# A hybrid decoder trunk on one core: the order of every engine planned by a list scheduler, and four blocks of seven products per feed-forward

## The chip, the core and the metric

The kernel runs on one core of a Trainium2 chip. A core has a matrix engine (TensorE, in the profile PE, with weight loads as PEld), a vector engine (VectorE, DVE), a scalar engine (ScalarE, ACT), GpSimd (POOL) and SyncE (SP), each with an instruction queue of its own that runs strictly in order, and 16 DMA engines. Work on one engine waits for another by semaphores. The metric is the device time of one execution in microseconds, the median of several runs.

## What is computed

Two layers. Each normalizes, runs a SwiGLU feed-forward, adds half of its normalized result, runs a mixer of three head groups in parallel, adds its normalized result, and runs a second feed-forward. Everything is float32: 256 tokens, width 1,024, feed-forward width 2,816.

```
for l in range(2):
    f = swiglu(rmsnorm(h, ff1_norm_pre[l]), ff1_w_gate[l], ff1_w_up[l], ff1_w_down[l])
    h = h + 0.5 * rmsnorm(f, ff1_norm_post[l])
    m = hybrid_mixer(rmsnorm(h, mix_norm_pre[l]), w_in[l], ...)   # state space | pooling | attention, then w_out
    h = h + rmsnorm(m, mix_norm_post[l])
    f = swiglu(rmsnorm(h, ff2_norm_pre[l]), ff2_w_gate[l], ff2_w_up[l], ff2_w_down[l])
    h = h + 0.5 * rmsnorm(f, ff2_norm_post[l])

swiglu(h, wg, wu, wd) = (silu(h @ wg) * (h @ wu)) @ wd
```

Most of the work is the four feed-forwards, three matrices of 1,024 x 2,816 each.

## The kernel before

**Float32 by three passes.** Each float32 operand is split into a high part `hi` (a copy rounded to the matrix engine's fast float32 type, made by ACT, line 104) and a low part `lo` = raw - hi (made by DVE, line 105). A product is hi x hi + hi x lo + lo x hi, three matmuls. Activations are split once; every weight is split once too, so ACT and DVE touch each weight that PE uses.

**Units, jobs and buffers.** Weights come in units of 128 x 2,048 float32 (1 MB). `Weights.load` (line 77) issues a unit's load from SP into one of four `raw` buffers; a job (`split_next`) makes a `hi` and a `lo` tile from it in two pieces of 1,024 columns (four of 512 for the first units), with five such pairs of tiles. `pump`, called at chosen points of the program, loads and splits ahead as long as buffers are free, and thereby sets the order on SP, ACT and DVE; the order of PE is that of the program.

**The feed-forward.** The 2,816 columns are eleven blocks of 256. Blocks 0 and 1 (`FIRST`) are made row tile by row tile (128 tokens) while the norm of the second row tile is still under way. Blocks 4, 7 and 10 (`PAIRS`) are plain: gate and up, 48 matmuls with 256 columns each (`mm_feat`, line 300). The blocks 2-3, 5-6 and 8-9 (`QUADS`) use a product of two-by-two blocks with seven multiplications in place of eight: with the tokens in two halves and the width in two halves, `ffn_quad` makes seven products of 12 matmuls with 512 columns (`product`, line 430) and combines them with a few additions of PSUM banks (lines 451 to 472). Its weights are g1 (gate, upper half of the rows), g2 (gate, lower half), u1 and u2 (up), and sums of them: T1 = g1 + u1, T2 = T1 + u2, T3 = u1 + u2, T4 = T2 + g2. T1, T2 and T4 are made by DVE in place in g1's raw buffer (line 101); for T3 the unit u2 is loaded a second time from POOL, by a DMA that adds to what lies in u1's buffer (line 103). The result h0, h1 comes with tokens on partitions and is turned by PE transposes (`turn_h`, line 405); a pair's result needs no turning. After each block the down product of the blocks before it runs (`mm_rows`, line 336: 12 matmuls with 512 columns for a unit and row tile).

**The mixer** is a chain of many smaller steps on all engines between products with `w_in` and `w_out`.

**What sets the order.** Instructions are recorded in program order, and each engine runs its own in that order, but where `tc.issue_after` moves a few at the start.

Of the kernel before, what the change touches and what calls it, by code (L numbers as in the profile page):

```python
# [17 lines left out]
P = 128  # L18
# [28 lines left out]

class Weights:
# [3 lines left out]
    def __init__(self, nc, rawp, splitp):  # L52
        self.nc, self.rawp, self.splitp = nc, rawp, splitp
        self.units, self.raw, self.jobs, self.parts = [], {}, [], {}
        self.loaded = self.live = self.split = self.held = 0

    def unit(self, src, cols=UNIT):
        self.units.append((src, cols))
# [8 lines left out]
    def plan(self, src, cols=UNIT, pieces=2):  # L67
        u = self.unit(src, cols)
        return self.job(u, free=(u,), pieces=pieces)

    def load(self, pieces=1):
        i = self.loaded
        src, cols = self.units[i]
        t = self.rawp.tile([P, KD * QDT], F32, tag="raw", name=f"raw{i}")
        step = cols // pieces
        for c in range(0, cols, step):
            self.nc.sync.dma_start(t[:, c : c + step], src[:, c : c + step])
        self.raw[i] = t
        self.loaded += 1
        self.live += 1  # L80

    def ready(self):
        u, sum_of = self.jobs[self.split][:2]
        return max(u, *(sum_of[::2] if sum_of else (u,))) < self.loaded

    def split_next(self, only=None):
# [4 lines left out]
        if i not in self.parts:  # L91
            self.parts[i] = [self.splitp.tile([P, KD * QDT], F32R, tag=x, name=f"{x}{i}") for x in ("hi", "lo")]
        hi, lo = self.parts[i]
        step = cols // pieces
        for c in range(0, cols, step):
            if only and c // step not in only:
                continue
            s = slice(c, c + step)
            if sum_of:
                x, op, y = sum_of  # L100
                nc.vector.tensor_tensor(raw[:, s], self.raw[x][:, s], self.raw[y][:, s], op=op)  # L101
                if add and c + step == cols:
                    nc.gpsimd.dma_start(self.raw[add[0]][:, :cols], add[1], accum_op=ALU.add)
            nc.scalar.activation(hi[:, s], raw[:, s], AF.Copy)  # L104
            nc.vector.tensor_tensor(lo[:, s], raw[:, s], hi[:, s].bitcast(F32), op=ALU.subtract)  # L105
# [32 lines left out]
def hybrid_trunk_kernel(ctx: ExitStack, tc: tile.TileContext, a, out: bass.AP):  # L138
    nc = tc.nc
    consts = ctx.enter_context(tc.tile_pool(name="consts", bufs=1))  # L140
    rawp = ctx.enter_context(tc.tile_pool(name="rawp", bufs=RAW_BUFS))
    splitp = ctx.enter_context(tc.tile_pool(name="splitp", bufs=SPLIT_BUFS))
    tmp = ctx.enter_context(tc.tile_pool(name="tmp", bufs=1))
    small = ctx.enter_context(tc.tile_pool(name="small", bufs=6))
    psum = ctx.enter_context(tc.tile_pool(name="psum", bufs=4, space=bass.MemoryType.PSUM))

    ids = iter(range(10**6))

    def buf(dtype=F32, n=512, tag="t"):
# [48 lines left out]
    gains = consts.tile([P, 2, D], F32, name="gains")  # L198
    xT = [consts.tile([P, KD, S], F32R, name=f"xT{i}") for i in range(2)]
# [5 lines left out]
    def split_into(dst, at, src_f32):  # L205

        hi, lo = dst[0][at], dst[1][at]
        split_into.last = nc.scalar.activation(hi, src_f32, AF.Copy)  # L208
# [867 lines left out]
```

## Time and profile before

| what | us |
|---|---|
| median of 3 runs | 950.46 (949.59 to 950.59) |
| the profiled execution | 950.96 |
| its span, first to last instruction | 949.3 |
| the last two matmuls of the program start | 942.5 |

The profile tells of one execution. A group row reads: line, engine, operation, tiles written and read (buffer numbers left out), shapes, count, then busy time and mean duration of one in ns, and the idle time before it with what ended it. A timeline row has the start, the length from the first start to the last end, and the count of merged equal instructions; in brackets the idle time just before it. Instructions of one engine overlap in their last part, so n equal ones in a row take n - 1 steps and one duration, and a step is shorter than a duration.

### The profile page before, as it was taken

The page shows a single profiled execution, that of the slowest core. Times are in us where ns is not written, and L with a number is a line of the kernel's source. Part 1 is how long each engine was busy: PE and PEld are TensorE (multiplying, and loading weights), DVE is VectorE, ACT ScalarE, POOL GpSimd, SP SyncE. Part 2 cuts the span into 40 slices and gives each one's busy share as a digit, 9 for nine tenths or more (in the row PEclk, how much of TensorE's full clock was granted, in tenths as well). Part 3 has the DMA queues.
Part 4 walks back from the last instruction along what each step waited for, and adds up shares of the span by engine and source line. Part 5 has one row for each costly group of instructions (what it writes and reads, how often), then busy time and mean ns, then how long its engine had stood idle before and what let it go on. Part 6 is the DMA issues. An engine that isn't in the chain of part 4 may idle for free.

```text
span 949.3 us, 13147 instructions
## 1 busy us (share of the span) xinstructions
PE 929.7 (98%) x5066; PEld 794.9 (84%) x5066; DVE 789.8 (83%) x1067; ACT 580.5 (61%) x923; POOL 34.7 (4%) x47
## 2 busy tenths in 40 slices
PE   7999999999999999999999999999999999999997
PEld 4779898988988789898887888898898887989896
DVE  6899898588887998998589989786888799989772
ACT  7576656468737565747467666556685566665651
POOL 0000000010001000000010000000000110000000
PEclk9999999999999999999999999999999999999999
DMA  8667666656243476758454958583733263858531
GB/s 315 214 243 244 241 203 248 242 175 224 96 177 124 110 297 198 294 145 307 179 186 124 346 143 310 139 313 126 268 132 133 89 195 123 331 175 285 172 117 45
DMA packets 28003, 190.56 MB, mean 201 GB/s; under 512 B 3106, under 2 KB 3362, under 8 KB 5924
## 3 DMA queue, kind: packets, MB, share of 16 engines
q1 hardware_dynamic: 26212, 177.13, 51.0%
q0 software_dynamic: 1728, 12.58, 7.2%
q8 instruction: 40, 0.66, 0.3%
q14 instruction: 23, 0.19, 0.1%
HBM read 188.65 MB, written 1.05 MB: 200 GB/s over the span
## 4 chain that ended last, share of the span: by engine, by line
PE 71%; DVE 11%; ACT 7%; issue 4%; POOL 1%; DMA 1%; POOLq 0%; DVEq 0%; ACTq 0%
PE acc L336 25%; PE wk L430 22%; PE wk L300 18%; DVE lo L105 5%; ACT hi L104 2%; PE wk L319 2%; ACT n L225 2%; POOL s L219 1%; DVE raw L101 1%; PE wk L405 1%; ACT n L669 1%; DMA raw<-in_ff_q 1%; DVE xT L209 1%; DVE n L209 1%; PE wk L866 1%
## 5 line engine op out<-in xcount | busy, mean ns | idle before, releaser
L105 DVE TENSOR_TENSOR lo<-raw,hi 128x1024 fp32r<-128x1024 f32 (+2 forms) x440 | 468.1, 1102 | 62.5 <-ACT hi L104 61.9
L104 ACT ACTIVATE hi<-raw 128x1024 fp32r<-128x1024 f32 (+2 forms) x440 | 399.4, 959 | 176.9 <-PE wk L300 37.5
L336 PE MATMUL acc<-hi,t 128*128 128x512 f32 x832 | 221.5, 396 | 3.0 <-ACT hi L104 2.9
L336 PEld LDWEIGHTS acc<-hi,t 128*128 128x128 f32 x832 | 154.3, 189 | 37.4 <-ACT hi L104 3.7
L300 PE MATMUL wk<-xT,hi 128*128 128x256 f32 x1088 | 144.0, 285 | 0.0
L300 PEld LDWEIGHTS wk<-xT,hi 128*128 128x128 f32 x1088 | 136.8, 192 | 2.3 <-issue 0.7
L336 PE MATMUL acc<-lo,t 128*128 128x512 f32 x416 | 115.4, 391 | 1.5 <-DVE lo L105 1.5
L319 PE MATMUL wk<-hi,xT 128*128 128x512 f32 x384 | 102.1, 398 | 2.5 <-ACT xT L208 1.4
L430 PE MATMUL wk<-hi,n 128*128 128x512 f32 x384 | 100.4, 390 | 0.0
L336 PEld LDWEIGHTS acc<-lo,t 128*128 128x128 f32 x416 | 77.9, 188 | 19.2 <-DVE lo L105 2.8
L319 PEld LDWEIGHTS wk<-hi,xT 128*128 128x128 f32 x384 | 71.8, 190 | 20.5 <-ACT hi L104 3.1
L101 DVE TENSOR_TENSOR raw<-raw,raw 128x1024 f32<-128x1024 f32 x72 | 86.3, 1217 | 1.7 <-DMA raw<-in_ff_q 1.6
L430 PEld LDWEIGHTS wk<-hi,n 128*128 128x128 f32 x384 | 71.9, 188 | 15.5 <-issue 0.8
L430 PE MATMUL wk<-hi,xT 128*128 128x512 f32 x288 | 76.9, 391 | 0.0
L300 PE MATMUL wk<-xT,lo 128*128 128x256 f32 x544 | 76.9, 284 | 0.0
L300 PEld LDWEIGHTS wk<-xT,lo 128*128 128x128 f32 x544 | 70.3, 192 | 0.0
L430 PEld LDWEIGHTS wk<-hi,xT 128*128 128x128 f32 x288 | 53.8, 188 | 11.1
L319 PE MATMUL wk<-lo,xT 128*128 128x512 f32 x192 | 52.9, 396 | 1.0 <-DVE lo L105 1.0
L208 ACT ACTIVATE t<-wk 128x256 fp32r<-128x256 f32 x72 | 26.9, 375 | 42.0 <-DVE t L209 22.1
L430 PE MATMUL wk<-lo,n 128*128 128x512 f32 x192 | 51.3, 389 | 0.0
L233 DVE TENSOR_TENSOR n<-acc,gains 128x512 f32<-128x512 f32 x24 | 16.5, 688 | 35.9 <-ACT n L225 35.9
L319 PEld LDWEIGHTS wk<-lo,xT 128*128 128x128 f32 x192 | 36.1, 189 | 9.8 <-DVE lo L105 2.2
(172 smaller groups left out, 763.1 us busy)
## 6 DMA issues: line engine op xcount, KB each, us to landing
raw<-in_ff_q SPq DMA_DIRECT2D x48, 1024.0 KB, 5.0
raw<-in_ff_d SPq DMA_DIRECT2D x44, 1024.0 KB, 5.1
raw<-in_ff_f SPq DMA_DIRECT2D x16, 1024.0 KB, 5.7
raw<-in_ff_q POOLq DMA_DIRECT2D x12, 1024.0 KB, 8.0
raw<-in_ff_g SPq DMA_DIRECT2D x12, 1024.0 KB, 4.8
raw<-in_ff_u SPq DMA_DIRECT2D x12, 1024.0 KB, 5.0
raw<-in_w_in SPq DMA_DIRECT2D x10, 1024.0 KB, 4.9
raw<-in_w_kvz SPq DMA_DIRECT2D x8, 1024.0 KB, 6.2
```

The lines of the kernel that those rows point to most:

```text
L101: nc.vector.tensor_tensor(raw[:, s], self.raw[x][:, s], self.raw[y][:, s], op=op)
L104: nc.scalar.activation(hi[:, s], raw[:, s], AF.Copy)
L105: nc.vector.tensor_tensor(lo[:, s], raw[:, s], hi[:, s].bitcast(F32), op=ALU.subtract)
L208: split_into.last = nc.scalar.activation(hi, src_f32, AF.Copy)
L209: nc.vector.tensor_tensor(lo, src_f32, hi.bitcast(F32), op=ALU.subtract)
L219: nc.gpsimd.tensor_tensor(r, v, halfexp, op=ALU.pow)
L225: nc.scalar.activation(junk, x, AF.Square, scale=1.0 / (gain * math.sqrt(n)), accum_out=ssq)
L233: nc.vector.tensor_tensor(fg[i], f[i], gains[:, 1, i * 512 : (i + 1) * 512], op=ALU.mult)
L300: nc.tensor.matmul(ps, w[:, k, s], y[:, k, :], start=i == 0 and k == 0, stop=i == 2 and k == KD - 1)
L319: m = nc.tensor.matmul(ps, y[:, k, :], w[:, k, :], start=h == 0 and n == 0, stop=h == 1 and n == len(parts) - 1)
L336: nc.tensor.matmul(acc[b], x[:, j, s], w[:, j, b * 512 : (b + 1) * 512], start=first and j == 0 and i == 0, stop=last and j == 1 and i == 2)
L430: nc.tensor.matmul(ps, x[:, k, :], w[:, k, :], start=first and n == 0, stop=n == len(parts) - 1, skip_group_check=not first)
```

## The change

**Planned order.** The program is no longer issued as it is written. All engine calls go to a `Planner`, which notes for each which tiles (and which parts of them) it reads and writes, gives it a cost by formulas, and then runs a list scheduler over all five engines at once: it repeatedly takes the engine whose next choice starts first, and of that engine's ready operations (within 20 ns of the earliest) the one with the earliest due time. Due times run backwards from the time at which PE would need each operation if PE ran without a gap in program order. It also hands out the buffers. The kernel then emits the plan; `pump` and its look-ahead are gone.

**Blocks.** `QUADS` becomes (2, 4, 6, 8) and `PAIRS` (10,): four blocks of seven products and one pair in each feed-forward. In a block the order is g1, T1, g2, a down unit, T3, T2, a down unit, u2, T4. T2 is made like T3, by an accumulating load: after T1 is split, u2 is loaded onto it. So u2 is read three times, T1 and T4 remain additions on DVE.

**Pieces and buffers.** Splits and additions are done in one piece of 2,048 columns, but for the first units of a stage. Pairs of split tiles go from five to six, the 512-wide working buffers `t` from 22 to 14.

```diff
-RAW_BUFS = 4
-SPLIT_BUFS = 5
+PEKEY = 0
+PAD = 300.0
+TMP, NBUF, ROUNDS = 14, 8, 1
+RAW_BUFS = 4
+PF, FINE = 2, 'g1 T1 g2'.split()
+AHEAD = "".split()
+ORDER = "g1 0 T1 1 g2 d T3 T2 d u2 T4".split()
+SUMMED = "T3 T2".split()
+SPLIT_BUFS = 6
 TAIL = 4
-FIRST, QUADS, PAIRS = (0, 1), (2, 5, 8), (4, 7, 10)
+FIRST, QUADS, PAIRS = (0, 1), (2, 4, 6, 8), (10,)
...
+class Planner:
...
+    def arrange(self, target=None):
...
+        for o in reversed(ops):
+            o.late = -1e9 if o.rush else min([target.get(o.n, end)] + [q.late - g for q, g in post[o.n]])
...
+        def pick(e):
+            best = [(s, o) for o in hand[e] if (s := earliest(o)) is not None]
...
+            first = min(s for s, _ in best)
+            now = [(o.n if e == "tensor" and PEKEY else o.late, o.n, s, o) for s, o in best if s <= first + 20]
+            late, _, s, o = min(now)
...
+            if o.kind == "dma":
+                line = max(s + (600 if e == "sync" else 1500), line) + o.tail * (1 if e == "sync" else 1.5)
+                done = line + o.tail * (0 if e == "sync" else 0.5) + 1700.0
...
 class Weights:
...
-    def job(self, unit, sum_of=None, free=(), pieces=2, add=None):
+    def job(self, unit, sum_of=None, free=(), pieces=1, add=()):
...
-                if add and c + step == cols:
-                    nc.gpsimd.dma_start(self.raw[add[0]][:, :cols], add[1], accum_op=ALU.add)
             nc.scalar.activation(hi[:, s], raw[:, s], AF.Copy)
             nc.vector.tensor_tensor(lo[:, s], raw[:, s], hi[:, s].bitcast(F32), op=ALU.subtract)
-        if only and pieces - 1 not in only:
-            return
+        for v, src in add:
+            nc.gpsimd.dma_start(self.raw[v][:, :cols], src, accum_op=ALU.add)
...
-    def pump(self):
...
+        def block(i, src, before):
+            names = "g1 u1 g2 u2".split()
...
+                add = []
+                if s in order[:3]:
+                    t = order[order.index(s) + 1]
+                    if t in SUMMED and not (t == "T1" and "T1" in AHEAD):
+                        add.append((u[k], S_[chain[t]]))
+                if s == "T1" and "T3" in SUMMED:
+                    add.append((u["u1"], S_["u2"]))
+                p[s, i] = W.job(u[k], (u[k], ALU.add, u[y]) if y else None, free=free, add=add, pieces=PF if i == QUADS[0] and s in FINE else 1)
...
+        for s in ORDER:
+            if s in "01":
+                turn(int(s))
+            elif s == "d":
+                if downs:
+                    downs.pop(0)()
...
+    for _ in range(ROUNDS):
+        target = nc.arrange(target)
...
+    with tc.manual_schedule():
+        nc.emit(tc.nc, sbuf, psum)
```

Three places show the new order. In the changed kernel every instruction has the line of `emit`, 354; a tile's first number is its place among the tiles of its name.

**POOL, first feed-forward of layer 0.** Before: the two norms' powers of the start, the three accumulating loads into u1's buffer (one a block), the next norm.

```order
L219 TENSOR_TENSOR s12_121<-s13_123,halfexp_85 128x1
L219 TENSOR_TENSOR s25_165<-s26_167,halfexp_85 128x1
L103 DMA raw5_190<-in_ff1_q 128x2048
L103 DMA raw15_572<-in_ff1_q 128x2048
L103 DMA raw24_986<-in_ff1_q 128x2048
L219 TENSOR_TENSOR s123_1625<-s124_1627,halfexp_85 128x1
```

Now:

```order
L354 TENSOR_TENSOR s14_120<-s13_118,halfexp0_63 128x1
L354 TENSOR_TENSOR s19_236<-s18_231,halfexp0_63 128x1
L354 DMA raw5_189<-in_ff1_q 128x2048
L354 DMA raw4_162<-in_ff1_q 128x2048
L354 DMA raw11_524<-in_ff1_q 128x2048
L354 DMA raw10_507<-in_ff1_q 128x2048
L354 DMA raw17_758<-in_ff1_q 128x2048
L354 DMA raw16_742<-in_ff1_q 128x2048
L354 DMA raw23_982<-in_ff1_q 128x2048
L354 DMA raw22_967<-in_ff1_q 128x2048
L354 TENSOR_TENSOR s114_1502<-s113_1496,halfexp0_63 128x1
```

Each block has two loads in a row: first into u1's buffer (T3), then into g1's (T2).

**DVE, around T2's combination of a block.** Before, in the third block of the first feed-forward, from T4's addition (raw23 is g1's buffer, lo34 is T4, lo32 T3, t98 the working tile into which T2's product goes):

```order
L101 TENSOR_TENSOR raw23_954<-raw23_954,raw26_1030 128x1024 x2
L105 TENSOR_TENSOR lo32_1221<-raw24_986,hi32_1220 128x1024 x2
L105 TENSOR_TENSOR lo33_1253<-raw26_1030,hi33_1252 128x1024 x2
L105 TENSOR_TENSOR lo34_1289<-raw23_954,hi34_1288 128x1024 x2
L105 TENSOR_TENSOR lo35_1301<-raw25_1008,hi35_1300 128x1024 x2
L451 TENSOR_TENSOR t98_1271<-wk101_1308,t98_1271 128x512
L105 TENSOR_TENSOR lo36_1324<-raw27_1226,hi36_1323 128x1024
L452 TENSOR_TENSOR wk99_1273<-wk99_1273,t98_1271 128x512
```

Now, in the second block of the first feed-forward (raw10 is g1's buffer, lo20 the split of u2, t15 takes T2's product, lo21 is T4, lo22 the next block's g1, raw16 its buffer):

```order
L354 TENSOR_TENSOR raw10_507<-raw10_507,raw12_537 128x2048
L354 TENSOR_TENSOR lo20_753<-raw15_700,hi20_731 128x2048
L354 TENSOR_TENSOR t15_640<-wk20_737,t15_640 128x512
L354 TENSOR_TENSOR wk17_630<-wk17_630,t15_640 128x512
L354 TENSOR_TENSOR wk19_720<-wk19_720,t15_640 128x512
L354 TENSOR_TENSOR lo21_785<-raw10_507,hi21_756 128x2048
L354 TENSOR_TENSOR lo22_797<-raw16_742,hi22_775 128x2048
L354 TENSOR_TENSOR t20_693<-t20_693,wk19_720 128x512
L354 TENSOR_TENSOR raw16_742<-raw16_742,raw17_758 128x2048
```

And in the second block of the second feed-forward (raw57 is g1's buffer, lo79 u2, lo80 T4, t107 takes T2's product, raw63 the next block's g1):

```order
L354 TENSOR_TENSOR raw57_2973<-raw57_2973,raw59_3017 128x2048
L354 TENSOR_TENSOR lo79_3236<-raw62_3157,hi79_3199 128x2048
L354 TENSOR_TENSOR t111_3215<-wk75_3183,t110_3195 128x2x128
L354 TENSOR_TENSOR lo80_3259<-raw57_2973,hi80_3238 128x2048
L354 TENSOR_TENSOR lo81_3271<-raw63_3222,hi81_3256 128x2048
L354 TENSOR_TENSOR raw63_3222<-raw63_3222,raw64_3240 128x2048
L354 TENSOR_TENSOR t107_3154<-wk77_3268,t107_3154 128x512
L354 TENSOR_TENSOR wk74_3160<-wk74_3160,t107_3154 128x512
L354 TENSOR_TENSOR wk76_3248<-wk76_3248,t107_3154 128x512
```

Before, DVE had T3 to u2 split before T2's combination. In the first feed-forward the next block's T1 addition (raw16 += raw17) now stands behind T2's combination (t15) and T4's split, in the second ahead of the combination (t107).

**DVE at the start.** Before, from the first split (raw0 to raw3 are the first four units, h is x, n27 and n28 the scaled second row tile):

```order
L105 TENSOR_TENSOR lo0_131<-raw0_105,hi0_130 128x512
L209 TENSOR_TENSOR xT1_104<-wk16_134,xT0_103 128x4x128
L209 TENSOR_TENSOR xT1_104<-wk17_141,xT0_103 128x4x128
L105 TENSOR_TENSOR lo0_131<-raw0_105,hi0_130 128x512 x3
L105 TENSOR_TENSOR lo1_181<-raw1_107,hi1_180 128x512
L214 TENSOR_SCALAR s24_164<-s21_159 128x1
L105 TENSOR_TENSOR lo1_181<-raw1_107,hi1_180 128x512
L251 SCALAR_TENSOR_TENSOR n27_170<-h_73,s25_165,acc5_110 128x512
L251 SCALAR_TENSOR_TENSOR n28_171<-h_73,s25_165,acc6_111 128x512
L105 TENSOR_TENSOR lo1_181<-raw1_107,hi1_180 128x512 x2
L105 TENSOR_TENSOR lo2_193<-raw2_174,hi2_192 128x512 x4
L105 TENSOR_TENSOR lo3_205<-raw3_176,hi3_204 128x512 x4
```

Now (n10 and n11 are the scaled second row tile):

```order
L354 TENSOR_TENSOR lo0_135<-raw0_82,hi0_122 128x512 x4
L354 TENSOR_TENSOR xT10_160<-wk1_129,xT00_137 128x4x128
L354 TENSOR_TENSOR lo1_166<-raw1_86,hi1_149 128x512 x4
L354 TENSOR_TENSOR xT10_160<-wk2_139,xT00_137 128x4x128
L354 TENSOR_TENSOR lo2_196<-raw2_90,hi2_173 128x512 x4
L354 TENSOR_SCALAR s17_220<-s15_210 128x1
L354 TENSOR_TENSOR lo3_222<-raw3_94,hi3_199 128x512 x4
L354 SCALAR_TENSOR_TENSOR n10_252<-h0_65,s19_236,acc0_105 128x512
L354 SCALAR_TENSOR_TENSOR n11_263<-h0_65,s19_236,acc1_116 128x512
```

The second row tile's scaling moved behind all sixteen splits of the first four units; on SP its load moved behind the four units' loads, of which two stood ahead of it before.

More of the change, by code (lines that the diff above doesn't have):

```diff
@@ L45 @@
 R_ALL = R_SN + 512
-class Weights:
[L52 to L58, printed above, removed]
+GRAIN, BANKS = 8, ("wk", "acc")
+ENGINES = ("vector", "scalar", "tensor", "gpsimd", "sync")
+LAG = {("scalar", "vector"): 33.0, ("scalar", "scalar"): 123.0, ("scalar", "gpsimd"): 80.0, ("vector", "scalar"): 33.0,
+       ("vector", "vector"): 84.0, ("vector", "gpsimd"): 144.0, ("gpsimd", "gpsimd"): 84.0, ("gpsimd", "vector"): 34.0, ("gpsimd", "scalar"): 34.0,
+       ("tensor", "vector"): 0.0, ("tensor", "scalar"): 0.0}
@@ new lines, with __init__, view @@
+class Tile:
+    def __init__(self, tag, shape, dtype):
+        self.tag, self.shape, self.dtype, self.index = tag, shape, dtype, None
+        self.real, self.uses, self.left, self.reads, self.writes, self.slot, self.end = None, 0, 0, [], [], None, 0.0
+    def view(self):
+        return View(self, (), np.arange(math.prod(self.shape[1:])).reshape(self.shape[1:]), (0, self.shape[0]))
+class Op:
+    __slots__ = ("n", "engine", "name", "args", "kw", "pre", "tiles", "late", "busy", "tail", "kind", "start", "rush")
@@ L59, in unit, with __init__, plan @@
+class Weights:
+    def __init__(self, nc):
+        self.nc, self.units, self.raw, self.jobs, self.parts = nc, [], {}, [], {}
+        self.loaded = self.split = 0
+    def unit(self, src, cols=UNIT, add=()):
+        self.units.append((src, cols, add))
         return len(self.units) - 1
-    def job(self, unit, sum_of=None, free=(), pieces=2, add=None):
+    def job(self, unit, sum_of=None, free=(), pieces=1, add=()):
         self.jobs.append((unit, sum_of, free, pieces, add))
         return len(self.jobs) - 1
-    def plan(self, src, cols=UNIT, pieces=2):
+    def plan(self, src, cols=UNIT, pieces=1):
@@ L68, in plan, with load @@
         u = self.unit(src, cols)
         return self.job(u, free=(u,), pieces=pieces)
-    def load(self, pieces=1):
+    def load(self):
         i = self.loaded
[L73 to L77, printed above, removed]
+        src, cols, add = self.units[i]
+        t = self.nc.tile([P, KD * QDT], F32, "raw")
+        self.nc.sync.dma_start(t[:, :cols], src[:, :cols])
+        for x in add:
+            self.nc.gpsimd.dma_start(t[:, :cols], x, accum_op=ALU.add)
@@ L78, in load, with get @@
         self.raw[i] = t
         self.loaded += 1
[L80 to L86, printed above, removed]
+    def get(self, i):
+        while i >= self.split:
+            u, sum_of = self.jobs[self.split][:2]
+            while max(u, *(sum_of[::2] if sum_of else (u,))) >= self.loaded:
+                self.load()
+            self.split_next()
+        return self.parts[i]
```

506 lines of the change are left out of this document (374 added, 132 removed).

## The prediction, made before the changed kernel had run

> **What bounds the kernel now.** I read the page from the top: busy time, then the chain that ended last, then the stretches of the span, then PE's waits.
>
> ```profile
> span 949.3 us, 13147 instructions
> PE 929.7 (98%) x5066; PEld 794.9 (84%) x5066; DVE 789.8 (83%) x1067; ACT 580.5 (61%) x923; POOL 34.7 (4%) x47
> PE 71%; DVE 11%; ACT 7%; issue 4%; POOL 1%; DMA 1%; POOLq 0%; DVEq 0%; ACTq 0%
> ...
> 10.00:25.00 15.00, 12.64 (x39) 8.12 (x40) 13.26 (x22) 14.59 (x28) 0.88 (x1) 0.89 0.93 359
> ...
> 45.00:55.00 10.00, 7.06 (x26) 5.15 (x25) 7.46 (x10) 7.19 (x11) 0.00 (x0) 0.83 0.46 163
> 55.00:120.00 65.00, 65.00 (x337) 55.86 (x336) 59.26 (x61) 42.37 (x49) 0.88 (x1) 1.00 0.72 250
> ...
> 330.00:480.00 150.00, 149.48 (x811) 129.06 (x810) 125.83 (x142) 91.05 (x126) 3.15 (x4) 1.00 0.64 225
> ```
>
> The columns of a stretch are its length, then busy time of PE, weight load, DVE, ACT and POOL, PE's granted clock, DMA share and GB/s. From 55 us on PE is full: 65.00 of 65, 149.48 of 150. Only the first 55 us have holes, 12.64 of 15 and 7.06 of 10, and only there the clock falls (0.89, 0.83). So after the first 55 us time comes from fewer or shorter matmuls alone, and any wait that the new order makes on PE costs its full length. The second engine matters as much: DVE has 59.26 of 65, 91%, in a stretch where PE never waits.
>
> ```profile
> PE acc L336 <- ACT hi L104: 2.9, 1, 2.9
> ...
> PE acc L714 <- ACT t L702: 1.6, 2, 0.8
> ...
> PE wk L319 <- ACT xT L208: 1.4, 5, 0.4
> ```
>
> The longest wait of PE is one of 2.9 us (at 48.9, first feed-forward); behind the start, the mixers' largest is 1.6 in two.
>
> **Part 1: four blocks of seven products.** In each of the four feed-forwards one more block replaces two pairs. The chain in order of time gives both:
>
> ```profile
> 123.15 5.75 PE wk L300 x48
> ...
> 135.54 11.08 PE acc L336 x48
> 146.61 19.09 PE wk L430 x84
> ```
>
> A pair is two matrices of 48 matmuls, 11.5 us; two pairs 23.0. A block is 84 matmuls, 19.09. The block's result also has to be turned, 8 more transposes:
>
> ```profile
> 128.75 0.60 PE L405 MATMUL wk<-ident,t 128*128 128x128 f32 x4
> 129.10 2.16 PE L300 MATMUL wk<-xT,hi 128*128 128x256 f32 x16
> ```
>
> Four transposes hold PE for 129.10 - 128.75 = 0.35, eight for 0.70. Saved: 23.0 - 19.09 - 0.70 = 3.21 per feed-forward, **12.8 us** in four. PE is full, so this counts in full unless a new wait eats it.
>
> **Part 2: DVE and ACT with 2,048-wide pieces.** Steps come from runs of equal instructions, where the last one's duration is taken off:
>
> ```profile
> L105 DVE TENSOR_TENSOR lo<-raw,hi 128x1024 fp32r<-128x1024 f32 x344 | 406.6, 1218 | 58.6 <-ACT hi L104 58.0
> ...
> L105 DVE TENSOR_TENSOR lo<-raw,hi 128x512 fp32r<-128x512 f32 x88 | 56.6, 683 | 3.9 <-ACT hi L104 3.9
> L209 DVE TENSOR_TENSOR t<-wk,t 128x256 fp32r<-128x256 f32 x72 | 29.8, 419 | 6.3 <-ACT t L208 5.7
> ...
> 46.00 5.77 DVE L105 TENSOR_TENSOR lo<-raw,hi 128x1024 fp32r<-128x1024 f32 x5 [1.97 <-ACT hi L104]
> ...
> 11.52 1.88 DVE L105 TENSOR_TENSOR lo<-raw,hi 128x512 fp32r<-128x512 f32 x3
> ...
> L104 ACT ACTIVATE hi<-raw 128x1024 fp32r<-128x1024 f32 x344 | 344.9, 1052 | 163.8 <-PE wk L300 37.5 <-DVE raw L101 34.6 <-PE acc L336 31.1
> ...
> L104 ACT ACTIVATE hi<-raw 128x512 fp32r<-128x512 f32 x88 | 50.0, 623 | 10.0 <-PE acc L336 4.0 <-DMA raw<-in_ff_f 3.1 <-issue 1.6
> ```
>
> DVE: (5.77 - 1.22) / 4 = 1.14 for 1,024 and (1.88 - 0.68) / 2 = 0.60 for 512, so 1.14 + 2 x 0.54 = 2.2 for 2,048 (by estimate; no such piece is in this trace). ACT's duration by the same line is 1.05 + 2 x 0.43 = 1.9. A block with its two down units now holds on DVE nine splits and two adds of 2.2 (24.2), six combinations of 0.60 (3.6) and four turned pieces of some 0.34 (1.4): 29.2. PE has 19.09 + 11.08 + 0.70, less overlaps: 30.8. DVE would be busy 95% where the old stretch had 91%. What hides it is the lead with which DVE enters a block, six split buffers deep.
>
> **Part 3: T2 and T3 by accumulating loads.** Three adds a block become two; one accumulating load becomes two, back to back on POOL's queue (32 in all for 12; the norms' POOL steps stand between the groups of eight, so none queues behind them).
>
> ```profile
> raw<-in_ff_q SPq DMA_DIRECT2D x48, 1024.0 KB, 5.0
> ...
> raw<-in_ff_q POOLq DMA_DIRECT2D x12, 1024.0 KB, 8.0
> ...
> q1 hardware_dynamic: 26212, 177.13, 51.0%
> q0 software_dynamic: 1728, 12.58, 7.2%
> ...
> 87.50:93.50 6.00, 6.00 (x28) 4.87 (x27) 6.00 (x9) 3.42 (x5) 0.00 (x0) 1.00 0.88 165
> ...
> 62.00:68.00 6.00, 6.00 (x28) 4.96 (x27) 6.00 (x7) 3.40 (x5) 0.00 (x0) 1.00 1.01 385
> ```
>
> An accumulating load lands after 8.0 and holds all DMA engines for 0.072 x 949.3 / 12 = 5.7 us, a plain one for 0.51 x 949.3 / 177.13 x 1.05 = 2.9. The stretch 87.5 to 93.5 is such a load alone (165 GB/s at a share of 0.88, against 385 in plain loads). No row shows two behind each other, or one beside a plain load. Six plain loads and two accumulating ones are 6 x 2.9 + 2 x 5.7 = 28.8 of DMA time in a block of 30.8: it fits, with little room. The four raw buffers hold, too: the next u1 goes into the one that T4's add frees, three splits and a turned piece (6.9) ahead of the T1 add, against 5.0 to landing. Counting from the end of T1's add: the first (T3) lands at 8.0; T1's split takes 1.9 + 2.2, so the second (T2) is issued at 4.2 and lands at 8.0 + 5.7 = 13.7 alone, at 16.6 if a plain load fits wholly in between. I take the middle, 15.2. T2's own hi and lo bring it to 19.3.
>
> What follows on DVE until the next block's T1 add is a fixed row. In the first feed-forward (rows of the order): lo of the down unit, T4's add, lo of u2, T2's combination and two subtractions, lo of T4 and of the next g1, one subtraction, the add: 6 x 2.2 + 4 x 0.6 = 15.6, so the cycle closes at **34.9 against PE's 30.8**. In the other three the T1 add stands ahead of the combination: 6 x 2.2 + 0.7 = 13.9, cycle 33.2. Those enter with a lead: the add is done by T2's end in block 1, so T2 of block 2 is ready 19.3 later and PE wants it 28.1 later (down 5.5, u2, T4, g1, T1, g2 at 2.7, turns 0.7, down 5.5, T3 2.7). Lead 8.8; three blocks lose at most 3 x 2.4 = 7.2. I take no wait of that kind there, and 0.2 a block for subtractions that stand behind a 2.2 us piece: +2.
>
> **The start.** All four first units are now loaded ahead of x's second half, the norm of which moves behind the splits on DVE and ACT.
>
> ```profile
> 8.37 0.75 DVE L251 SCALAR_TENSOR_TENSOR n<-h,s,acc 128x512 f32<-128x512 f32 x1 [0.76 <-PE acc L938]
> ...
> 9.71 0.69 DVE L105 TENSOR_TENSOR lo<-raw,hi 128x512 fp32r<-128x512 f32 x1 [0.59 <-ACT hi L104]
> ...
> 27.10 1.03 PE L260 MATMUL wk<-ident,n 128*128 128x128 f32 x8
> ...
> 28.39 1.20 PE L319 MATMUL wk<-hi,xT 128*128 128x512 f32 x4 [0.25 <-ACT xT L208]
> ...
> 48.86 3.80 PE L336 MATMUL acc<-hi,t 128*128 128x512 f32 x8 [2.94 <-ACT hi L104]
> ```
>
> Row tile 1 began at 28.39. DVE now has sixteen 512-wide splits and two turned pieces of 0.60 (10.8) from 9.7 on, and with the 1.7 that it idled between 10 and 25 (15 - 13.26) is through at 22.2; two scalings of 0.75, then transposes and evacuation, some 1.2, make 24.9. **-3** (0 to -5).
>
> **The first feed-forward** has no lead. DVE's rows up to T2's combination of block 1 are 34 pieces of 0.60, eight of 1.14, six of 2.2 and four of 0.34, 44 us from 8.4 on; with the 1.7 and some 3 of waiting for T2's load it is there at 57 to 58. PE's way there is 24.9 + 48 matmuls (10.9, by 19.09 / 84 each) + 19.7 = 55.5. So block 2 waits about 3 for T2, blocks 3 and 4 wait 34.9 - 30.8, 4 each: **+11** (0 if the second load lands at 13.7 and DVE is not late, 15 if at 16.6). The old wait of 2.94 at 48.9, and the slow clock behind it, (1 - 0.83) x 10 = 1.7, go: **-4.6**; the +11 stands in their place.
>
> Would the new waits slow the clock too? The row says that 2.94 us were enough. Mine are split, hi and lo arriving 2.2 apart with 0.9 of matmuls between, so I add nothing; whole they would add 1.7 each. The Trainium skill, "TensorE: Matmul & The Clock Gate", Part 1, has the half rate after an idle window of about 3.4 us. By that rule none of them would add anything; the 2.94 here is a little under its figure.
>
> **Mixers and norms**: their rows are re-ordered, with waits of 1.6, 1.4 and smaller to win. I take -3 (-6 to +6: nothing shows the new order's own waits).
>
> **Sum**: 950.96 (the profiled execution) - 12.8 - 3 - 4.6 + 11 + 2 - 3 = 940.6, a change of -10.4; the median of the runs is 0.5 lower: **940.0**.
>
> **Rivals.** *The cycle binds in every feed-forward* (slower). For it: DVE at 95%, and two loads in series where one was. Against: the lead of 8.8. It decides once T2's load lands more than about 17 us after T1's add, so that three blocks lose over 8.8. If the lead is not there at all, nine further blocks lose 3 to 4: 940.6 + 27 to 37 = 968 to 978; half of it 955. The Trainium skill, "DMA: Bandwidth & Descriptors", Issuing engines are not separate DMA queues, says that transfers of all issuing engines interleave on the same 16, which is how a plain load would stretch T2's; no run here shows the two together. *The waits vanish* (faster still): the second load lands at 13.7, DVE is not late in the first feed-forward, the mixers give 6: 940.6 - 11 - 2 - 3 = 924.6. *The new order gives back what the products save*: first feed-forward at 15, mixers at +4: 951 to 952.
>
> **How the numbers follow.** Forecast (930 to 948) 0.60, waits vanish 0.20, given back 0.08, cycle binds 0.12. Faster by over 0.2% (about what a measurement here can tell from no change) 0.80, within 0.07, slower 0.13. Range 924 to 957: the vanished waits below, half the binding cycle above.
>
> **What would show it.** 768 fewer 256-wide matmuls (eight pairs of 96), products still at 19.1 for 84; PE's waits in the first feed-forward stand on T2 (hi, then lo) and come from accumulating loads; in the other three PE stays full; DVE's 2,048 pieces step at 2.2; T2's loads land 13 to 17 after T1's add. Waits of 3 us on T2 in every block, or DVE ahead of PE everywhere, would prove me wrong.

## The result and the profile after

| | before | after |
|---|---|---|
| median of the runs, us | 950.03 (948.77 to 950.59) | 959.63 (955.12 to 963.02) |
| after to before | | 1.010, interval 1.0056 to 1.0144 |
| profiled execution, us (span) | 950.96 (949.3) | 959.03 (957.2) |

The kernel became slower by one per cent; the forecast was 940.0, in a range of 924 to 957. The head of the page of after: span, busy time, the two DMA queues, the chain that ended last by engine, and the accumulating loads (KB each, us to landing).

```profile
span 957.2 us, 12144 instructions
PE 924.6 (97%) x4666; PEld 768.8 (80%) x4666; DVE 806.0 (84%) x915; ACT 589.0 (62%) x799; POOL 54.0 (6%) x67
q1 hardware_dynamic: 26212, 177.13, 49.4%
q0 software_dynamic: 4608, 33.56, 18.4%
PE 32%; DVE 15%; DMA 11%; ACT 5%; issue 5%; DVEq 0%; POOLq 0%; POOL 0%; ACTq 0%
raw<-in_ff_q POOLq DMA_DIRECT2D x32, 1024.0 KB, 9.0
```

PE is busy only 5.1 us less (929.7 before), though 400 matmuls are gone, and of the chain that ended last it holds 32% where it held 71%. The rest is a ring: DVE, then a load that adds (DMA 11%, nearly all of it raw<-in_ff_q), then ACT's split, then DVE again. One turn of it, from the chain in order of time (start, length, what): a T1 add, T1's hi and lo, the load that makes T2, T2's hi.

```profile
593.79 2.30 DVE raw L354
596.19 1.92 ACT hi L354
598.14 2.30 DVE lo L354
...
600.84 10.21 DMA raw<-in_ff_q
611.14 1.93 ACT hi L354
```

Where the time went is read from the first turned pieces (rows wk<-ident,n of PE's timeline), which open each stage. Those of feed-forward 2 and of the mixer behind it, before and then after:

```profile
297.34 1.27 PE L260 MATMUL wk<-ident,n 128*128 128x128 f32 x8
...
478.40 1.03 PE L260 MATMUL wk<-ident,n 128*128 128x128 f32 x8
```

```profile
293.92 1.03 PE L354 MATMUL wk<-ident,n 128*128 128x128 f32 x8
...
481.02 1.03 PE L354 MATMUL wk<-ident,n 128*128 128x128 f32 x8
```

| stage | before, us | after, us | difference |
|---|---|---|---|
| up to row tile 1 | 27.1 | 21.5 | -5.6 |
| rest of feed-forward 1 | 170.2 | 174.3 | +4.1 |
| mixers 1 and 2 | 100.0 + 100.1 | 98.1 + 98.0 | -4.0 |
| feed-forward 2 | 181.1 | 187.1 | +6.0 |
| feed-forward 3 | 180.9 | 184.9 | +4.0 |
| feed-forward 4, to the end of the span | 189.9 | 193.3 | +3.4 |

So all the gain is at the start, up to row tile 1, and in the mixers. The feed-forwards, each of which has 3.2 us less of products, are all longer. One period of a block in the second feed-forward shows why. First the stretches from the end of one T1 add to the end of the next (length, then PE, weight load, DVE, ACT, POOL, granted clock, DMA share, GB/s):

```profile
343.40:377.50 34.10, 34.10 (x154) 27.73 (x152) 29.60 (x22) 19.94 (x17) 1.75 (x2) 1.00 0.80 244
377.50:411.40 33.90, 31.62 (x140) 25.18 (x140) 29.57 (x22) 19.82 (x17) 1.73 (x2) 1.00 0.81 248
```

Both last 34 us, and DVE works 29.6 of them. The second, on DVE's timeline (start, length, instruction; in brackets its idle time and what ended it):

```profile
385.13 2.28 DVE L354 TENSOR_TENSOR lo<-raw,hi 128x2048 fp32r<-128x2048 f32 x1
388.28 2.29 DVE L354 TENSOR_TENSOR lo<-raw,hi 128x2048 fp32r<-128x2048 f32 x1 [0.87 <-ACT hi L354]
...
394.77 4.49 DVE L354 TENSOR_TENSOR lo<-raw,hi 128x2048 fp32r<-128x2048 f32 x2 [3.26 <-ACT hi L354]
...
404.58 4.48 DVE L354 TENSOR_TENSOR lo<-raw,hi 128x2048 fp32r<-128x2048 f32 x2
409.10 2.29 DVE L354 TENSOR_TENSOR raw<-raw,raw 128x2048 f32<-128x2048 f32 x1
411.31 0.68 DVE L354 TENSOR_TENSOR t<-wk,t 128x512 f32<-128x512 f32 x1
412.02 1.30 DVE L354 TENSOR_TENSOR wk<-wk,t 128x512 f32<-128x512 f32 x2
```

And what ACT and PE do there:

```profile
386.33 1.92 ACT L354 ACTIVATE hi<-raw 128x2048 fp32r<-128x2048 f32 x1 [3.24 <-DMA raw<-in_ff_q]
392.82 1.92 ACT L354 ACTIVATE hi<-raw 128x2048 fp32r<-128x2048 f32 x1 [3.33 <-DMA raw<-in_ff_q]
```

```profile
402.56 2.04 PE L354 MATMUL wk<-hi,n 128*128 128x512 f32 x8
404.43 1.10 PE L354 MATMUL wk<-lo,n 128*128 128x512 f32 x4
405.37 1.09 PE L354 MATMUL wk<-hi,n 128*128 128x512 f32 x4
406.30 1.09 PE L354 MATMUL acc<-hi,t 128*128 128x512 f32 x4
...
412.78 1.20 PE L354 MATMUL wk<-hi,n 128*128 128x512 f32 x4 [0.84 <-DVE wk L354]
```

Two holes of DVE, 0.87 and 3.26, each end with a hi of ACT, and ACT had waited for the accumulating loads of T3 (386.33) and T2 (392.82). T2's own product waits for nothing: its lo is written by 397.0, PE takes T2 at 403.5 (the second four of the x8). It ends by 406.6. The combination behind it could follow, but DVE's row has two splits and the next block's T1 add ahead of it. It starts at 411.31, and PE's u2 (412.78) waits for its subtraction.

One more wait comes once in each of the last three feed-forwards, at the same place of the last block:

```profile
437.91 1.20 PE L354 MATMUL wk<-hi,n 128*128 128x512 f32 x4 [2.49 <-DVE t L354]
...
437.00:445.00 8.00, 7.09 (x24) 5.67 (x25) 5.96 (x6) 4.95 (x5) 0.00 (x0) 0.79 0.96 375
622.00:630.00 8.00, 7.20 (x24) 5.76 (x25) 5.98 (x6) 4.83 (x5) 0.00 (x0) 0.79 1.04 390
904.00:912.00 8.00, 6.80 (x23) 5.43 (x24) 6.24 (x6) 5.26 (x5) 0.00 (x0) 0.79 1.02 378
```

T3's product waits for a PSUM bank, out of which DVE still has to read the last turned piece of the block before (a transposed part of its result). In DVE's row that piece stands behind T4's add and a split:

```profile
432.95 2.28 DVE L354 TENSOR_TENSOR raw<-raw,raw 128x2048 f32<-128x2048 f32 x1
435.15 2.28 DVE L354 TENSOR_TENSOR lo<-raw,hi 128x2048 fp32r<-128x2048 f32 x1
437.35 0.42 DVE L354 TENSOR_TENSOR t<-wk,t 128x256 fp32r<-128x256 f32 x1
```

The three waits are 2.49, 2.47 and 2.11 us. The clock is lower behind each, 0.79 over 8 us: (1 - 0.79) x 8 = 1.7 us more, three times.

### The profile page after: what moved, and what is told of

Its sections match the earlier page's. It is cut to its first block, busy times and chain, and to the rows that moved or that the text cites. A ratio compares the mean times of both kernels' runs of the same rounds, so it can differ in the third digit from the quotient of the medians.

```text
span 957.2 us, 12144 instructions
## 1 busy us (share of the span) xinstructions
PE 924.6 (97%) x4666; PEld 768.8 (80%) x4666; DVE 806.0 (84%) x915; ACT 589.0 (62%) x799; POOL 54.0 (6%) x67
## 3 DMA queue, kind: packets, MB, share of 16 engines
q0 software_dynamic: 4608, 33.56, 18.4%
## 4 chain that ended last, share of the span: by engine, by line
PE 32%; DVE 15%; DMA 11%; ACT 5%; issue 5%; DVEq 0%; POOLq 0%; POOL 0%; ACTq 0%
PE wk L354 22%; DMA raw<-in_ff_q 11%; PE acc L354 10%; DVE lo L354 10%; ACT hi L354 5%; DVE raw L354 4%; DVE t L354 1%; DMA raw<-in_ff_d 1%; ACT t L354 0%; DVE h L354 0%; DVEq L1403 0%; DVE n L354 0%; POOLq L1403 0%; POOL s L354 0%; ACTq L354 0%
## 5 line engine op out<-in xcount | busy, mean ns | idle before, releaser
L354 DVE TENSOR_TENSOR lo<-raw,hi 128x2048 fp32r<-128x2048 f32 (+3 forms) x300 | 482.6, 1632 | 78.5 <-ACT hi L354 76.9
L354 ACT ACTIVATE hi<-raw 128x2048 fp32r<-128x2048 f32 (+3 forms) x300 | 406.5, 1386 | 226.6 <-DVE raw L354 91.1
L354 PE MATMUL wk<-hi,xT 128*128 128x512 f32 (+1 forms) x832 | 213.1, 387 | 5.2 <-DVE t L354 2.9
L354 ACT ACTIVATE t<-wk 128x512 f32<-128x512 f32 (+2 forms) x194 | 85.5, 480 | 41.6 <-PE wk L354 32.3
L354 PE MATMUL wk<-lo,xT 128*128 128x512 f32 (+1 forms) x416 | 108.3, 383 | 1.5 <-DVE lo L354 1.5
L354 DVE TENSOR_TENSOR t<-wk,t 128x256 fp32r<-128x256 f32 (+1 forms) x140 | 71.0, 517 | 14.5 <-ACT t L354 14.3
L354 PE MATMUL wk<-xT,hi 128*128 128x256 f32 x576 | 77.1, 284 | 0.0
L354 PEld LDWEIGHTS wk<-xT,hi 128*128 128x128 f32 x576 | 72.6, 191 | 1.6 <-issue 0.7
L354 DVE TENSOR_TENSOR raw<-raw,raw 128x2048 f32<-128x2048 f32 (+1 forms) x36 | 73.5, 2049 | 0.3
L354 PEld LDWEIGHTS wk<-lo,n 128*128 128x128 f32 x256 | 49.0, 193 | 15.1 <-DVE lo L354 3.2
L354 DVE TENSOR_TENSOR n<-acc,gains 128x512 f32<-128x512 f32 x24 | 16.5, 690 | 34.9 <-ACT n L354 34.9
```

Source lines behind the costliest of these rows:

```text
L354: getattr(getattr(nc, o.engine), o.name)(*map(put, o.args), **{k: put(v) for k, v in o.kw.items()})
```

## The experiments

Ratios are to the kernel before on the same chip. The changed kernel stands at 959.63, and all runs below but the seventh are edits of it; the seventh is one of the kernel before. "Period" is the time from one T1 add to the next, the last two of the second feed-forward in the profiled execution; holes are what DVE's busy time leaves of it.

| run | us | interval of the ratio | periods | DVE busy | holes |
|---|---|---|---|---|---|
| after | 959.63 | 1.0056 to 1.0144 | 34.1, 33.9 | 29.6, 29.6 | 4.5, 4.3 |
| 1 T2 by DVE | 971.88 | 1.0203 to 1.0252 | 36.9, 36.0 | 32.4, 31.7 | 4.5, 4.3 |
| 2 combination first | 953.56 | 1.0024 to 1.0068 | 34.2, 34.5 | 29.7, 30.2 | 4.5, 4.2 |
| 3 five raw buffers | 956.91 | 1.0052 to 1.0082 | 33.1, 34.9 | 29.4, 30.2 | 3.7, 4.7 |
| 5 down unit split early | 974.69 | 1.0230 to 1.0287 | 37.0, 36.5 | 31.0, 30.1 | 6.0, 6.4 |
| 12 pieces of 1,024 | 974.82 | 1.0211 to 1.0315 | 34.5, 35.3 | 30.0, 30.1 | 4.4, 5.3 |
| 13 six raw buffers | 954.89 | 1.0029 to 1.0075 | 33.2, 35.1 | 29.4, 30.1 | 3.8, 5.0 |
| 14 = 13 + 5 | 951.76 | 0.9993 to 1.0025 | 34.2, 32.0 | 29.5, 29.5 | 4.7, 2.5 |
| 11 = 13 + 5 + 2 | 952.81 | 1.0003 to 1.0047 | 31.6, 31.6 | 29.5, 29.5 | 2.1, 2.1 |

The interval of the changed kernel overlaps with those of runs 2, 3 and 13, so their gains are not clear of the noise. Runs 1, 5 and 12 are clearly slower than it, 11 and 14 clearly faster.

**1. T2's sum by DVE again.**

```diff
-SUMMED = "T3 T2".split()
+SUMMED = "T3".split()
```

> T2's sum is made by DVE again (one more add of 2.2 us a block), only T3 stays an accumulating load. Theory A (the cycle through the second accumulating load sets the pace: T1's add, load of T3, load of T2 behind it, T2's split, the rest of DVE's row, the next T1 add, 33.9 us where PE has 30.8): the cycle is gone, DVE's busy time of 29.7 + 2.2 = 31.9 us is the pace, 2 us a block less in the twelve blocks behind each feed-forward's first: 940 to 950 us. Theory B (DVE simply has too much to do, or its 2,048-wide pieces stand in the way, and the load doesn't matter): 12 to 16 more pieces of 2.2 us on the path, 975 to 995 us.

971.88: between the two, nearer to B. Taking the second load out of the ring gave nothing; the holes are as large as before (they now stand at the chain of the T2 add: DVE waits 2.0 for the sum's hi), and the add's 2.2 us lengthen the period by as much. So the load is not the pace by itself. The pace is DVE's row: its work and the holes that its fixed order leaves.

**2. Combination ahead of the add.**

```diff
-                nc.vector.tensor_tensor(pc, pc, w2, op=ALU.subtract)
+                W.behind = [nc.vector.tensor_tensor(pc, pc, w2, op=ALU.subtract)]
...
+                if fence:
+                    o.pre.update((b, "ORDER") for b in self.behind)
```

(`fence` is set for T1's job alone.)

> The next block's T1 add is held until the first two combinations behind T2 (the sum into t and the subtraction from T1's bank) have been issued on DVE; nothing else is changed. Theory A (the cycle through the second load): the waits of u2 on the subtraction go, but the T1 add comes some 2 us later and so does T2's load, the cycle becomes 35 to 36 us and eats the 6 us that T2 had in hand after two blocks: 955 to 970 us. Theory B (only the place of the combination behind the add costs, DVE's 4 us of idle time a block are enough): the waits of 1.3, 0.8, 2.6 us go, 8 to 20 us less: 940 to 951 us.

953.56, some 6 us better by the medians: between the two. In the last three feed-forwards u2 waits little or not at all in the second block (0, 0.6, 0 by PE's steps beyond the median of their form), and the wait of 2.5 on a bank is gone. But the periods are 34.2 and 34.5, as before, so the same subtraction is late a block further on: 1.8, 2.3 and 1.7 in the third, 1.1, 2.1 and 2.1 in the fourth. The place costs some 6 us; the period stays.

**3. Five raw buffers**, five split buffers instead of six.

```diff
-RAW_BUFS = 4
+RAW_BUFS = 5
-SPLIT_BUFS = 6
+SPLIT_BUFS = 5
```

> A fifth raw buffer (split buffers 5 instead of 6 to make room). Theory A: the next block's two units are loaded without waiting for T4's add, so the T1 add can stand earlier in DVE's row, the lead grows, and the waits on DVE shrink: 940 to 952 us; T1's add should be followed by T2's split within 20 us as before, but by the next T1 add within 31 to 33. Theory B (DVE's work or the split buffers are the limit): no gain or a loss, 957 to 975 us.

956.91, 2.7 us better, which is within the noise, periods 33.1 and 34.9: neither. More room alone doesn't close the holes.

**4. Small tiles padded** (see the end for why).

```diff
-    halfexp = keep([P, 1], F32, "halfexp")
+    halfexp = keep([P, 16], F32, "halfexp")[:, :1]
...
-        row = keep([P, R_ALL], F32, "row")
+        row = keep([P, R_ALL + 8], F32, "row")[:, :R_ALL]
```

> Two small tiles are made larger (halfexp 16 columns, the row constants 8 columns more) so that the n tiles lie at a multiple of 64 bytes like the split weights; the order is the same but for what the planner does with it. If the 7 ns that each of the 768 matmuls with a stationary n tile takes longer than before (234 against 227) come from the place of the two operands against each other: 227 again and up to 5.4 us less, 954 to 957 us with the waits as they are (less, where PE's wait only grows). If they come from something else: 234 still and 959 us.

961.25 (1.0095 to 1.0140) and 232 to 234 ns: a multiple of 64 bytes isn't it.

**5. The second down unit split ahead of T2.**

```diff
+SPLITS = "g1 T1 g2 d T3 d T2 u2 T4".split()
...
-            steps = [s for s in ORDER if s not in "01"]
+            steps = SPLITS
```

> Only the order in which units are split changes: the block's second down unit is split ahead of T2 (g1 T1 g2 d T3 d T2 u2 T4); PE's order of the program is as in the changed kernel. Theory A (period of a block = DVE's busy 29.6 us plus the 4 us in which its in-order row stands behind the split of T3 and of T2, whose loads are late): a ready split of 2.2 us fills the hole, the period falls from 33.9 to 31.5 to 32.5 us, 1.4 to 2.4 us in each of the 12 blocks behind a first one: 930 to 945 us. Theory B (the holes belong to the chain add, hi, lo on ACT and DVE and move elsewhere, as they did when T2's sum went back to DVE): period 33 to 34 still, 952 to 962 us.

974.69: worse than either theory said. The hole moved and grew. On DVE, then on ACT:

```profile
412.43 4.49 DVE L355 TENSOR_TENSOR lo<-raw,hi 128x2048 fp32r<-128x2048 f32 x2 [4.56 <-ACT hi L355]
```

```profile
410.48 5.53 ACT L355 ACTIVATE hi<-raw 128x2048 fp32r<-128x2048 f32 x3 [3.02 <-DMA raw<-in_ff_d]
```

The down unit was not ready. With four raw buffers its load is issued only when the first down unit's lo is done:

```profile
401.02 2.28 DVE L355 TENSOR_TENSOR lo<-raw,hi 128x2048 fp32r<-128x2048 f32 x1
...
403.37 0.33 SPq L355 DMA_DIRECT2D raw<-in_ff_d  x1
```

It lands 7.1 us later (410.48), beside T2's accumulating load, and T2's split stands behind it and is late in its turn. (My expectation of run 11 below says 10 us; it is 7.1.)

**6. n tiles at the top of SBUF** (an own pool behind the others).

```diff
-pool = psum if t.tag in BANKS else sbuf
+pool = psum if t.tag in BANKS else npool if t.tag == "n" else sbuf
```

> The n tiles lie behind all others in SBUF (as high as they lay in the kernel before, 158 to 174 KB there, 212 to 228 KB here) instead of ahead of the weights (9 to 26 KB); the order of the work is the same. If the place is what costs 7 ns in each of 768 matmuls with a stationary n tile: 227 ns again, up to 5.4 us less, 953 to 957 us. If not: 234 ns still, 958 to 963 us.

962.71 (1.0094 to 1.0176) and 230 to 235 ns: the height isn't it.

**7. Four blocks in the old order** (an edit of the kernel before).

```diff
-FIRST, QUADS, PAIRS = (0, 1), (2, 5, 8), (4, 7, 10)
+FIRST, QUADS, PAIRS = (0, 1), (2, 4, 6, 8), (10,)
```

> The kernel before with one edit: blocks at 2, 4, 6, 8 and one pair at 10 (part 1 alone, in the hand-written order, 1,024-wide pieces, T2's and T4's sums on DVE). Theory A (four blocks in a row leave DVE no time to catch up; its work in a block is then 9 splits and 3 adds of 2.28 and 5 us of small ones, 32.4 us, and stalls come on top): 12.8 us of products saved, 12 blocks that lose 2 to 5 us each: 962 to 998 us. Theory B (the scheduler's order is what loses, the hand-written one would keep PE full): 937 to 945 us.

1041.73 (1.0945 to 1.0981), beyond A. The stretch is one period; the waits are PE's in the whole run (total, times, longest):

```profile
411.00:449.00 38.00, 30.46 (x130) 24.64 (x130) 33.03 (x35) 21.67 (x26) 0.86 (x1) 0.91 0.68 219
...
PE wk L405 <- DVE t L472: 67.5, 12, 7.9
```

DVE works 33.0 of 38.0, PE waits 4 to 8 us in every block behind the first, twelve times, and its clock falls to 0.91. So part 1 alone costs 91 us in the old order; the new order and the loads win most of that back.

**8. Three blocks, three pairs, all else as changed.**

```diff
-FIRST, QUADS, PAIRS = (0, 1), (2, 4, 6, 8), (10,)
+FIRST, QUADS, PAIRS = (0, 1), (2, 5, 8), (4, 7, 10)
```

> The changed kernel with the blocks as before (2, 5, 8, and pairs at 4, 7, 10): scheduler, 2,048-wide pieces and both accumulating loads, without part 1. Theory A (DVE catches up in the 11.5 us of a pair between two blocks, so that its period doesn't reach PE): what the start (5), the mixers (4) and the wait at 48.9 (4.6) give remains, less 576 x 7 ns = 4 us of longer matmuls: 938 to 947 us. Theory B (the scheduler's order costs in every block by itself, whatever follows it): 950 to 960 us.

942.6 (0.9906 to 0.9942): faster than both kernels, as A has it. From one T1 add to the next there is now a block and a pair:

```profile
352.30:403.70 51.40, 51.40 (x289) 44.78 (x288) 38.05 (x27) 27.15 (x22) 1.73 (x2) 1.00 0.73 232
```

PE is full for 51.40; DVE has 13.4 us left, and holes of that size cost nothing. This is the run that decides: the scheduler's order, the wide pieces and the two loads are all there, and the loss is gone from the last three feed-forwards. What PE's steps lose there in waits (those of over 0.25 us, beyond the median step) is 0.4 us in each, where the changed kernel has 7.2, 5.1 and 4.7; in the first feed-forward 4.0 of 8.8 are left. The loss came from four blocks in a row.

**9. All behind the row constants 96 bytes higher.**

```diff
-        row = keep([P, R_ALL], F32, "row")
+        row = keep([P, R_ALL + 24], F32, "row")[:, :R_ALL]
```

> The row constants get 24 columns (96 bytes) more, so that all tiles allocated behind them start 96 bytes higher. n tiles and split weights then lie at the same offset within 512 bytes (160), as they did in the kernel before (416 for n, hi, lo, xT and t); in the changed kernel it is 160 for n and 64 for the weights, in the two tries before 192 and 128, 192 and 64. The order is the same. If this offset sets the 7 ns: 227 ns in the 768 matmuls with a stationary n tile and up to 5.4 us less, 953 to 958 us. If not: 232 to 234 ns, 958 to 963 us.

958.75 (1.0078 to 1.0111): the step is 227 again in most runs of matmuls (230 in some), PE's busy time falls (919.4 for 924.6), and the time is hardly less. PE saved 5 us, and its waits by the profile grew by 4 (30.0 for 25.8): the period was DVE's.

**10. The same with three blocks.**

> Three blocks and three pairs as in the eighth run, with the 96 bytes of the ninth. If the offset sets the 7 ns, 576 x 7 ns = 4 us come off a kernel in which PE hardly waits: 937.5 to 940 us. If not: 942 to 944 us. Either way it says nothing on the chain of the blocks.

940.78 (0.9883 to 0.9927), about 2 us less than without; a little beyond the 940 that was expected, and the intervals overlap.

**11. Six raw buffers, early split, combination first, 96 bytes.**

> Four blocks again, with all that should shorten a block's period together: six raw buffers (five split buffers), the second down unit split ahead of T2, the combination ahead of the next T1 add, and the 96 bytes. In the fifth run the down unit split early had itself a late load (10 us to landing, beside T2's accumulating load, since its buffer came free only with the first down unit's split); six buffers take that away. Theory A (holes of 4 us in DVE's row, each from a load that starts late, set the period; DVE's work alone would fit into PE's 30.8): period 31 to 32.5 us, 935 to 948 us. Theory B (DVE's order has no room: its chain add, hi, lo and the adds' places leave 4 us of holes wherever the loads land): period 33.5 to 35 us, 950 to 965 us.

Period 31.6, as A has it, with PE full. But the profiled execution took 946.85 us, the shortest of five, which is in A's range; the median, 952.81, is in B's, and no trace shows an execution of that length.

```profile
346.30:377.90 31.60, 31.60 (x145) 26.16 (x144) 29.49 (x23) 19.77 (x17) 1.75 (x2) 1.00 0.82 258
377.90:409.50 31.60, 31.60 (x145) 26.15 (x144) 29.51 (x23) 19.83 (x17) 1.74 (x2) 1.00 0.86 268
```

So the holes can be closed: in that execution the second feed-forward falls to 178.1 us (187.1 changed, 181.1 before). It doesn't hold everywhere: the first still has a wait of 5.7 us at 158, and in the third and fourth some periods are 34 again, with holes of 4.4 and 4.6. Why these differ, I haven't found; what PE waits for by this profile is still DVE for the most part, 18.0 of 23.5 us in eleven waits for an instruction that writes t.

**12. Pieces of 1,024 throughout.**

> The changed kernel with 1,024-wide pieces everywhere (part 2 undone alone, order by the same scheduler). 11 splits and adds a block take 2.28 instead of 2.2 us (0.9 us more on DVE) and ACT's by as much more, but a chain add, hi, lo of two pieces is 1.7 us shorter, and the second load is issued sooner. Theory A (the holes set the period): the shorter chain wins, 945 to 957 us. Theory B (DVE's amount of work sets it): 12 x 0.9 = 11 us more, 965 to 975 us.

974.82, as B has it, 15 us worse than the changed kernel. DVE's work in a period rises by only 0.4 to 0.5 and the holes by up to 1.0; the rest is ACT, which now brings banks free late, as PE's waits show (the changed kernel has none on ACT t):

```profile
PE wk L354 <- ACT t L354: 17.5, 7, 3.8
```

Part 2 is a gain here, though not by DVE's work alone, as I had it in B.

**13 and 14. Which of the three edits closes the holes.** 13 is 3 with six buffers and the 96 bytes; 14 adds the early split of 5.

> Of the four edits of the eleventh run only two: six raw buffers (five split buffers) and the 96 bytes. Splits in the changed kernel's order, the next T1 add free to stand ahead of the combination. Theory A (the holes come from loads that start late, for want of a free raw buffer): the period stays near the 31.6 us of the eleventh run, T2's split waits less: 944 to 953 us. Theory C (the holes come from the order, T2's split ahead of the ready down unit: T2's own load still lands 15 us behind the T1 add): period 33 to 34 us as in the changed kernel and with five buffers, 954 to 960 us.

> Six raw buffers, the second down unit split ahead of T2, the 96 bytes; the next T1 add is not held behind the combination. Theory C (order and buffers only work together: the down unit is split in the hole, and its load isn't late): period 31.5 to 32.5 us as in the eleventh run, 946 to 954 us, so that the fence gives little. If the fence was what made the eleventh run: 955 us or more, period 33 or more.

13: 954.89, periods 33.2 and 35.1: the buffers alone leave the holes (C), though the time is 0.4% under that of run 9, which has the 96 bytes alone (intervals 1.0029 to 1.0075 and 1.0078 to 1.0111). 14: 951.76, periods 34.2 and 32.0, holes smaller in most blocks: the early split, which cost 15 us with four buffers (5), gives another 0.4% with six. The fence of 2 adds nothing measurable to them (11).

**15. Three blocks with six raw buffers and the 96 bytes.**

> Three blocks and three pairs with six raw buffers (five split buffers) and the 96 bytes. Theory A and C alike: DVE isn't late here but in the first feed-forward (waits of 1.5 at 62 and 2.8 at 84), so earlier loads can give 0 to 4 us and one split buffer less can cost as much: 936 to 943 us. If the raw buffers were the limit here too, below 936 us.

938.98 us, ratio 0.9876 (0.9859 to 0.9893): the fastest of all, 1.2% under the kernel before.

## Why the prediction was wrong, point by point

- **Part 1, -12.8: right as matter of PE.** 400 matmuls fewer; with the 96 bytes in both, the steps of all matmuls add up to some 12 us less with four blocks (run 9) than with three (run 10): each matmul by the median step of its form.
- **Part 2: right.** Three 2,048-wide pieces in a row last 6.70 in run 1, one 2.28: a step of 2.21 (forecast 2.2). ACT's take 1.92 (1.9). A block's work on DVE is 29.6 (29.2).
- **Part 3: right in size.** T2's load is there 15.4 us after the T1 add's end (377.46 to ACT's start at 392.82; forecast 15.2), its lo 19.6 after (19.3), the period 33.9 (33.2).
- **The start, -3:** -5.6, beyond its bound of -5. **The mixers, -3:** -4.0.
- **First feed-forward, +11: right in size, wrong in place, so the size is luck.** Step by step beyond each form's median, PE's matmuls lose 10.7 us from 55 on (0.9 before). They stand at lo of g1 and T1 and at u2's subtraction; only one, of 0.4 at 155.0 on its lo, is at T2.
- **The step that failed: "Lead 8.8; three blocks lose at most 3 x 2.4 = 7.2. I take no wait of that kind there", costed at +2.** By the same count the last three feed-forwards lose 10.8, 8.6 and 8.2 us, where before had 2.9, 2.7 and 2.6: +19.4. The lead was measured where it is large. T2 kept its 6 us in hand; but PE waits for other parts of DVE's row as well, and there the lead was gone after one period. PE's next product, u2, waits for the combination, which DVE does behind the next T1 add: 4.4 us in the three, and 3.2 more at the product behind u2, which waits for DVE's next subtraction. The greater part is the bank in the last block: 7.6, and 5.0 by the slower clock behind it. I had the order in the row ("the T1 add stands ahead of the combination") and used it to shorten the cycle, not to ask who waits for what was pushed back. With a ring of 33.9 against PE's 31 or so, the consumer with the least in hand sets when it starts to cost. Run 2 puts the place of the combination at some 6 us; runs 11 and 14 show that the period itself had holes to close, and run 8 that a pair behind each block pays for all of it there.
- **The clock.** "Mine are split ... so I add nothing": the three waits of 2.1 to 2.5 us on a bank were whole, and behind each stand 1.7 more; part of the 19.4. The rule of the Trainium skill, "TensorE: Matmul & The Clock Gate", Part 1 (half rate after an idle window of about 3.4 us), would have added nothing here. The trace decides against it: 2.11 were enough. The length of the wait alone doesn't decide either. In run 14 a wait of 2.74 us (to 443.46) left the clock at 1.00, and one of 1.96 (to 905.01) was followed by 0.79:

```profile
442.00:450.00 8.00, 6.54 (x33) 5.61 (x34) 7.29 (x9) 2.00 (x2) 0.00 (x0) 1.00 0.91 345
904.00:912.00 8.00, 6.99 (x27) 5.77 (x28) 6.07 (x8) 1.68 (x1) 0.00 (x0) 0.79 0.04 15
```

- **Not in the sum at all: +5.4.** 768 products' matmuls with a stationary n tile took 234 ns a step for 227.
- With these the sum closes: 940.6 - 2.6 (start) - 1.0 (mixers) - 1.2 (first feed-forward, 10.7 - 0.9 for 11) + 17.4 (the other three, 19.4 for 2) + 5.4 = 958.6, against 959.03.
- **The rivals.** "The cycle binds in every feed-forward" is what happened, at half its price (955 forecast, 959.6 measured, of which the longer steps are 5.4), but not at the point that I gave: T2's load landed at 15.4, not beyond 17. Its chance of 0.12 hung on the same wrong consumer.

## What to carry to other kernels

A lead is worth what its least consumer has: list everything that waits for an engine's row, not only the transfer that was changed, and ask for each how long it has in hand. When a second engine needs 95% of the first one's time in a repeated block, the holes of its in-order row count in full, and cheap-looking work for the first engine (here the pairs) may be what lets the second catch up. The early split was worth something only with the buffers; tried alone, it looked harmful.

## What the runs showed of the hardware

**Where two operands lie against each other costs 3%.** Matmuls with a stationary n tile and a moving hi or lo (fp32r, 512 wide) step at 227 ns in the kernel before and at 234 in the changed one. PE's timeline of before, of after, and of run 9, four matmuls a row:

```profile
354.53 1.07 PE L430 MATMUL wk<-lo,n 128*128 128x512 f32 x4
355.44 1.07 PE L430 MATMUL wk<-hi,n 128*128 128x512 f32 x4
```

```profile
347.17 1.09 PE L354 MATMUL wk<-lo,n 128*128 128x512 f32 x4
348.10 1.10 PE L354 MATMUL wk<-hi,n 128*128 128x512 f32 x4
```

```profile
349.88 1.07 PE L354 MATMUL wk<-lo,n 128*128 128x512 f32 x4
350.79 1.07 PE L354 MATMUL wk<-hi,n 128*128 128x512 f32 x4
```

0.91 us for four before, 0.93 after, 0.91 with 96 bytes between. The instructions are the same; the tiles' places in SBUF are not. In the built programs both operands start at the same offset within 256 bytes in the kernel before (160 and 160) and in runs 9, 10 and 11 (160 and 160), and differ in the changed kernel (n 160, weights 64) and in runs 4 (192, 128) and 6 (192, 64). The texts of the runs speak of 512 bytes; but a split tile takes 8,448 bytes, so that about half of them start 256 bytes further than they say (in the kernel before at 160 beside 416, with n at 416), and nearly all matmuls there step at 227 all the same. xT and t lie with the weights in all of them, and their matmuls take 227 throughout. That the offset decides is shown by run 9, which keeps the order and moves the weights by 96 bytes against n; what in the chip makes it so isn't.

**Two accumulating loads queue up.** Issued 4 us apart, the second landed 6.5 us behind the first (386.33 and 392.82), about the 5.7 that one holds the DMA engines (7.2% of 949.3 us for twelve in the kernel before; 18.4% of 957.2 for 32, 5.5 each, in the changed one). A plain load beside them took 7.1 in run 5, where the median of the down units is 5.9.
